# Seven-product weight sums in a one-core decoder layer: from VectorE subtractions to transfers that add in SBUF

## The chip, the cores and the metric

One NeuronCore of a Trainium2 chip runs the whole kernel. The metric is device time of one execution in microseconds (us); lower is better. The names used for the engines are those of the profile: PE (TensorE), PEld (TensorE's weight loads), DVE (VectorE), ACT (ScalarE), POOL (GpSimd), SP (SyncE), the last of which only issues transfers here.

## What is computed

One decoder layer on 256 tokens of width 2048, in float32. What matters here is the start and the end of it:

```
proj = x @ w_in                      # queries, gates, RG-LRU input, merge gates g_a, g_b, ...
attn = sparse_attention(...)         # 16 heads
branch_a = (attn * silu(attn_gate)) @ w_branch_a
branch_b = (rglru(...) * silu(rnn_gate)) @ w_branch_b
merged = sigmoid(g_a) * branch_a + sigmoid(g_b) * branch_b
x = layernorm(alpha * x + merged @ w_out)
```

The change concerns two column blocks of 512 of the merge gates: block 2 of g_a and block 3 of g_b, both products of x with 2048 x 512 pieces of w_in.

## The kernel before

Float32 products are made from three matmuls of float32r halves: `hi_of` (L115, on ACT) rounds a tile, `lo_of` (L119, on DVE) subtracts the rounded part. So every weight tile is loaded by SP into a buffer `raw` (four of them, 128 x 1024), rounded by ACT into `hi`, subtracted by DVE into `lo` (five of each), and only then used by PE. A buffer `raw` comes free when DVE has made the `lo`; SP waits for that before it issues the next load into it, and issues in program order. The list `halves` holds all weight tiles in the order of use. `load_to(n)` (L203) issues loads up to tile n, `split_to(n)` (L253) makes hi and lo; callers keep the splits about five tiles ahead of PE and the loads about nine.

The query projection runs over 32 column tiles, `single(i)`, i from 0 to 31, each with two weight tiles of kind `wt`. Attention of a head (`head(h)`) is laid between them in small steps, each in its place on the engines' queues. For each head SP loads a bias tile, POOL adds the causal mask to it (L563, two instructions), and DVE uses it (L623 and L625). DVE, ACT and POOL take their instructions strictly in program order, so an instruction that waits holds up everything behind it.

Behind most of the query tiles a step of the second seven-product group is inserted (a Strassen-like scheme: the two gate blocks are four 128-token by 1024-row by 512-column quarter products each way, computed with seven products instead of eight). The steps are j1 (k = 0 to 7), j2 (0 to 7), j3 (0 to 3), j4 (0 to 7), one for each query tile, each with one more entry in `halves`. Its weights are sums of quarters of the weight matrix, made on DVE by `sums` (L231) from what lies in `raw` and in eight lasting tiles `form[k]`, 128 x 512:

- j1: form = raw's second half - raw's first half (L240); the matrix `wj` holds both halves side by side
- j2: form = half of raw - form (L242)
- j3: raw = form - raw, in two halves (L246)
- j4: form = form - half of raw (L249)

`quarter_step` (L954) multiplies them with sums of x: SJ[1], SJ[2], SJ[4] are made before (`early_sums`), SJ[3] by four calls of `late_sum(j)` during the steps j2 and j3, as three additions on POOL each (L935 to L937) into a tile `s3d`, which ACT and DVE split. `after_j1` to `after_j4` combine the products in PSUM to the gate blocks.

Of the kernel before, what the change touches and what calls it, by code (L numbers as in the profile page):

```python
# [14 lines left out]
OP = mybir.AluOpType  # L15
# [76 lines left out]
def layer(ctx, tc, ar, out):  # L92
    nc = tc.nc
# [41 lines left out]
    def slot(name, dt=F32R, late=False):  # L135
        tag, bufs = ("late", 2) if late else ("slot", 14)
        return big.tile([P, 2 * T], dt, name=name, tag=tag, bufs=bufs)
# [44 lines left out]
    halves, where = [], {}  # L182
# [15 lines left out]
    NO = len(halves)  # L198
    halves += [("wo", ec, pc) for ec in range(4) for pc in range(8)]
    raws, parts = {}, {}  # L200
    st = {"load": 0, "split": 0}

    def load_to(n):  # L203
        while st["load"] < min(n, len(halves)):
            i = st["load"]
            kind, a, s = halves[i]
            st["load"] += 1
            if kind in ("s1b", "s2b") or kind in ("j2", "j4") and a % 2:
                continue
            if kind == "s1a":  # L210
                nc.sync.dma_start(form[a], ar["wgb"][0, 4 + a // 2, :, a % 2, :])
            raw = wpool.tile([P, 1024], F32, name=f"raw{i}", tag="raw", bufs=4)
            raws[i] = raw
            if kind == "wt":
                src = ar["wt"][a, :, s * 8:(s + 1) * 8, :].rearrange("p k c -> p (k c)")
            elif kind == "j1":
                src = ar["wj"][a].rearrange("p k c -> p (k c)")
            elif kind in ("j2", "j3", "j4"):
                src = {"j2": ar["wgb"][3, 4 + a // 2], "j3": ar["wga"][2, a], "j4": ar["wga"][2, 4 + a // 2]}[kind]
                src = src.rearrange("p k c -> p (k c)")  # L220
            elif kind in ("s1a", "s2a"):
                src = ar["ws"][a + (8 if kind == "s2a" else 0)].rearrange("p k c -> p (k c)")
            else:
                src = ar[kind][a, s].rearrange("p k c -> p (k c)")
            nc.sync.dma_start(raw, src)

    form = {}

    def sums(i):  # L231


        kind, k, _ = halves[i]
        if kind in ("j2", "j4") and k % 2:
            i = next(n for n in reversed(range(i)) if halves[n][:2] == (kind, k - 1))
        raw = raws[i]
        half = raw[:, k % 2 * 512:(k % 2 + 1) * 512]
        if kind == "j1":
            return nc.vector.tensor_sub(form[k], raw[:, 512:], raw[:, :512])  # L240
        if kind == "j2":
            return nc.vector.tensor_sub(form[k], half, form[k])  # L242
        if kind == "j3":
            for e in range(2):
                c = slice(e * 512, (e + 1) * 512)
                nc.vector.tensor_sub(raw[:, c], form[2 * k + e], raw[:, c])  # L246
            return
        if kind == "j4":
            return nc.vector.tensor_sub(form[k], form[k], half)  # L249
        nc.vector.tensor_sub(raw[:, 512:], raw[:, 512:], raw[:, :512])  # L250
        nc.vector.tensor_sub(form[k], form[k], raw[:, 512:])

    def split_to(n):  # L253
        while st["split"] < min(n, len(halves)):
            i = st["split"]
            kind, k, _ = halves[i]
            follower = halves[i + 1][0] if i + 1 < len(halves) else None
            if follower == "s1a":
                load_to(i + 2)
                sums(i + 1)  # L260
            load_to(i + 1)
            if NO + 24 <= i < NO + 28:
                raw = raws.pop(i)
                pieces = []
                for e in range(2):
                    late = i == NO + 27 and e == 1
                    hi, lo = slot(f"wh{i}_{e}", late=late), slot(f"wl{i}_{e}", late=late)
                    c = raw[:, e * 512:(e + 1) * 512]
                    hi_of(hi, c)
                    lo_of(lo, c, hi)  # L270
                    pieces.append((hi, lo))
                parts[i] = pieces
            else:
                if kind == "s1b":
                    raw = raws.pop(i - 1)
                    nc.vector.tensor_sub(raw[:, 512:], form[k], raw[:, :512])
                    src = [(slice(0, 512), form[k]), (slice(512, 1024), raw[:, 512:])]
                elif kind == "j1":
                    src = [(slice(0, 512), raws.pop(i)[:, :512]), (slice(512, 1024), form[k])]
                elif kind in ("j2", "j4"):  # L280
                    n = i if k % 2 == 0 else next(n for n in reversed(range(i)) if halves[n][:2] == (kind, k - 1))
                    raw = raws.pop(n) if k % 2 else raws[n]
                    src = [(slice(0, 512), raw[:, k % 2 * 512:(k % 2 + 1) * 512]), (slice(512, 1024), form[k])]
                elif kind == "s2b":
                    src = [(slice(0, 512), form[k])]
                else:
                    raw = raws[i] if kind == "s1a" else raws.pop(i)
                    src = [(slice(0, 1024), raw)]
                if kind == "s2a":
                    nc.vector.tensor_sub(form[k], form[k], raw[:, :512])  # L290
                hi = wpool.tile([P, 1024], F32R, name=f"hi{i}", tag="hi", bufs=5)
                lo = wpool.tile([P, 1024], F32R, name=f"lo{i}", tag="lo", bufs=5)
                for c, v in src:
                    hi_of(hi[:, c], v)
                for c, v in src:
                    lo_of(lo[:, c], v, hi[:, c])
                parts[i] = (hi, lo)
            if follower in ("j1", "j2", "j3", "j4"):
                load_to(i + 2)
                sums(i + 1)  # L300
            st["split"] += 1

    def mm(ps, w, rhs, high, start, stop):
# [369 lines left out]
    gates = {}  # L673
# [230 lines left out]
                    S[i + 1, 2 * j + e] = (dst[i][:, e, 0, :], dst[i][:, e, 1, :])  # L904


    SJ = {}

    def early_sums():

        x = yield from load_quarters(0)
        yield 8
        homes = {(s, j): slot(f"sj{s}_{j}").rearrange("p (k e t) -> p k e t", k=2, e=2)
                 for s, j in [(1, j) for j in range(4)] + [(s, j) for j in range(4) for s in (2, 4)]}
        for j in range(4):
            yield 2
            a11, a21, a12, a22 = four(x, j)
            v = {s: rows2(tmp_tile(f"sumj{j}_{s}", tag, 2)) for s, tag in ((1, "g"), (2, "g"), (4, "u"))}
            nc.vector.tensor_add(v[1], a21, a22)
            nc.vector.tensor_sub(v[2], v[1], a11)  # L920
            nc.vector.tensor_sub(v[4], a12, v[2])
            yield
            for s in v:
                hi_of(homes[s, j][:, :, 0, :], v[s])
            yield 2
            for s in v:
                lo_of(homes[s, j][:, :, 1, :], v[s], homes[s, j][:, :, 0, :])
                for e in range(2):
                    SJ[s, 2 * j + e] = (homes[s, j][:, e, 0, :], homes[s, j][:, e, 1, :])

    def late_sum(j):
# [16 lines left out]
        for i in range(2):  # L948
            SJ[3, 2 * j + i] = (hi[:, i, :], lo[:, i, :])

    psj = {}
    cq = {}

    def quarter_step(job, k):  # L954
# [4 lines left out]
        def a(row, t):  # L959
            return xs[:, row, t * P:(t + 1) * P], xs[:, row, T + t * P:T + (t + 1) * P]  # L960

        todo = {"j1": lambda: ((1, a(k, 0)), (5, SJ[1, k])),
                "j2": lambda: ((3, SJ[4, k]), (6, SJ[2, k])),
                "j3": lambda: ((7, SJ[3, 2 * k]), (7, SJ[3, 2 * k + 1])),
                "j4": lambda: ((2, a(8 + k, 0)), (4, a(8 + k, 1)))}[job]()
# [19 lines left out]
    def after_j2():  # L985

        cq["b"] = gates["ga", 2, 1] = gate_tile("ga2_1")
        nc.vector.tensor_add(cq["b"], psj[6], cq["a"])
        yield
        nc.gpsimd.tensor_add(cq["c"], cq["c"], cq["b"])  # L990
        yield 2
        gates["gb", 3, 0] = gate_tile("gb3_0")
        nc.vector.tensor_add(gates["gb", 3, 0], psj[3], cq["c"])

    def after_j3():

        nc.vector.tensor_add(cq["b"], psj[7], cq["b"])
        yield
        gates["gb", 3, 1] = gate_tile("gb3_1")
        nc.vector.tensor_add(gates["gb", 3, 1], psj[7], cq["c"])  # L1000

    def after_j4():

        c11 = gates["ga", 2, 0] = gate_tile("ga2_0")
        nc.vector.tensor_add(c11, psj[2], cq["a"])
        nc.vector.tensor_sub(cq["b"], cq["b"], psj[4])
        accs.insert(0, 3)
        auxs.append(7)
        yield 20
        for g in (c11, cq["b"]):  # L1010
            nc.scalar.activation(g, g, AF.Sigmoid)
            yield
# [338 lines left out]
    for ec in range(3):  # L1351
        pss = [acc_tile(f"pso{ec}_0"), aux_tile(f"pso{ec}_1")]
        for pc in range(8):
            n = NO + ec * 8 + pc
# [84 lines left out]
```

## Time and profile before

| | |
|---|---|
| median of 3 runs | 1013.32 us (1013.16 to 1013.74) |
| the profiled execution: its own time | 1013.73 us |
| its span in the profile | 1012.0 us |
| granted TensorE clock, mean | 0.998 of full speed |
| PE busy | 1004.2 us, 99% |
| DVE busy | 783.9 us, 77% |
| ACT busy | 597.6 us, 59% |
| POOL busy | 149.7 us, 15% |
| moved by transfers | 210.08 MB, mean 208 GB/s |

The profile is of one execution. The span runs from the first to the last instruction; the time measured from outside is 1.7 us longer. An engine's busy time leaves out waits and the issue of transfers. "lo<-raw" means an instruction that reads the tile raw and writes lo. The time from a transfer's issue to its landing holds its wait for the transfers ahead of it.

### The profile page before, as it was taken

What the parts mean: (1) busy time and instruction counts of PE and PEld (TensorE: products, weight loads), DVE (VectorE), ACT (ScalarE), POOL (GpSimd) and SP (SyncE); (2) the same over time, 40 slices, a digit from 0 to 9 for tenths busy, and PEclk for the clock granted to TensorE, in tenths of its full rate; (3) what the DMA queues carried; (4) which work ended last, traced back from release to release, by engine and by line L of the source; (5) the groups of instructions that cost most, each with busy time, mean ns of one, the idle gap of its engine ahead of it and who ended that gap; (6) DMA issues with size and microseconds to landing.
All of it is one profiled execution on the core that took longest, in us unless ns stands there. A gap on an engine that the chain in (4) does not pass through costs nothing.

```text
span 1012.0 us, 15050 instructions
## 1 busy us (share of the span) xinstructions
PE 1004.2 (99%) x5320; PEld 865.9 (86%) x5320; DVE 783.9 (77%) x1298; ACT 597.6 (59%) x1022; POOL 149.7 (15%) x182
## 2 busy tenths in 40 slices
PE   9999999999999999999999999999999999999997
PEld 8888888888888888888888888888888888888885
DVE  5578889778789988768888878888678876655685
ACT  5566656666666667566555555555985555444452
POOL 0015621110124210300000000000343320000002
PEclk9999999999999999999999999999999999999999
DMA  9745886776646565766666676555556668656652
GB/s 307 260 151 195 282 319 209 229 220 198 187 155 214 183 213 171 238 201 209 218 219 193 221 233 191 195 187 190 174 166 206 193 211 327 219 182 188 199 167 84
DMA packets 63915, 210.08 MB, mean 208 GB/s; under 512 B 6992, under 2 KB 14032, under 8 KB 62816
## 3 DMA queue, kind: packets, MB, share of 16 engines
q1 hardware_dynamic: 60512, 195.32, 60.2%
q0 software_dynamic: 2608, 12.88, 3.4%
q8 instruction: 42, 0.69, 0.3%
q10 hardware_dynamic: 720, 0.92, 0.3%
q14 instruction: 33, 0.27, 0.1%
HBM read 206.96 MB, written 6.32 MB: 211 GB/s over the span
## 4 chain that ended last, share of the span: by engine, by line
PE 97%; DVE 2%; issue 0%; ACT 0%; DVEq 0%; ACTq 0%
PE ps_q L306 16%; PE ps_ag L306 9%; PE ps_xr L306 9%; PE ps_rg L306 9%; PE ps_bb L1107 3%; PE ps_bb L1106 3%; PE ps_ba L1106 3%; PE ps_bb L1105 3%; PE ps_ba L1105 3%; PE ps_ba L1107 3%; PE psq L306 2%; PE ps_qi L306 2%; PE pso L1107 2%; PE pso L1106 2%; PE pso L1105 2%; PE ps_gb L1106 1%
## 5 line engine op out<-in xcount | busy, mean ns | idle before, releaser
L119 DVE TENSOR_TENSOR lo<-raw,hi 128x1024 fp32r<-128x1024 f32 (+1 forms) x348 | 416.2, 1202 | 179.2 <-ACT hi L115 175.3
L115 ACT ACTIVATE hi<-raw 128x1024 fp32r<-128x1024 f32 (+1 forms) x348 | 348.3, 1017 | 156.4 <-PE pso L1107 25.3
L306 PE MATMUL ps_q<-xs,hi 128*128 128x512 f32 x512 | 126.7, 391 | 0.0
L306 PEld LDWEIGHTS ps_q<-xs,hi 128*128 128x128 f32 x512 | 94.0, 188 | 18.2
L306 PEld LDWEIGHTS ps_q<-xs,lo 128*128 128x128 f32 x512 | 65.6, 191 | 2.5
L306 PE MATMUL ps_q<-xs,lo 128*128 128x256 f32 x512 | 66.4, 283 | 0.0
L563 POOL TENSOR_TENSOR bias<-bias,mask 128x256 f32<-128x256 f32 (+1 forms) x32 | 32.2, 1026 | 195.7 <-DMA bias<-dz 184.5
L306 PE MATMUL ps_ag<-xs,hi 128*128 128x512 f32 x256 | 60.0, 390 | 0.0
L306 PE MATMUL ps_xr<-xs,hi 128*128 128x512 f32 x256 | 59.6, 390 | 0.0
L306 PE MATMUL ps_rg<-xs,hi 128*128 128x512 f32 x256 | 59.5, 390 | 0.0
L306 PEld LDWEIGHTS ps_xr<-xs,hi 128*128 128x128 f32 x256 | 47.6, 188 | 9.6
L306 PEld LDWEIGHTS ps_rg<-xs,hi 128*128 128x128 f32 x256 | 47.6, 188 | 9.6
L306 PEld LDWEIGHTS ps_ag<-xs,hi 128*128 128x128 f32 x256 | 47.5, 188 | 9.5
L1105 PE MATMUL ps_bb<-hi,ub 128*128 128x512 f32 x128 | 50.4, 393 | 0.0
L1107 PE MATMUL ps_bb<-hi,ub 128*128 128x512 f32 x128 | 49.9, 390 | 0.0
L1106 PE MATMUL ps_bb<-lo,ub 128*128 128x512 f32 x128 | 49.8, 389 | 0.0
L1106 PE MATMUL ps_ba<-lo,ua 128*128 128x512 f32 x128 | 49.8, 389 | 0.0
L1107 PE MATMUL ps_ba<-hi,ua 128*128 128x512 f32 x128 | 49.8, 389 | 0.0
L1105 PE MATMUL ps_ba<-hi,ua 128*128 128x512 f32 x128 | 49.8, 389 | 0.0
L115 ACT ACTIVATE hi<-form 128x512 fp32r<-128x512 f32 x40 | 25.4, 634 | 28.0 <-PE ps_ba L1107 8.8
L778 POOL MEMSET xp<- 128x3 f32 x16 | 1.6, 101 | 254.0 <-ACT ga L1068 164.9
L1105 PE MATMUL pso<-hi,xs 128*128 128x512 f32 x96 | 37.5, 391 | 0.0
(409 smaller groups left out, 2135.2 us busy)
## 6 DMA issues: line engine op xcount, KB each, us to landing
raw<-in_wt SPq DMA_DIRECT2D x168, 512.0 KB, 4.7
raw<-in_wba SPq DMA_DIRECT2D x32, 512.0 KB, 3.8
raw<-in_wbb SPq DMA_DIRECT2D x32, 512.0 KB, 4.2
raw<-in_wo SPq DMA_DIRECT2D x32, 512.0 KB, 3.8
raw<-in_wga SPq DMA_DIRECT2D x24, 512.0 KB, 4.6
raw<-in_wgb SPq DMA_DIRECT2D x20, 512.0 KB, 4.7
raw<-in_ws SPq DMA_DIRECT2D x16, 512.0 KB, 4.3
wr<-in_wA SPq DMA_DIRECT2D x14, 424.0 KB, 4.9
```

The lines of the kernel that those rows point to most:

```text
L115: nc.scalar.activation(hi, src, AF.Copy)
L119: nc.vector.tensor_sub(lo, src, f(hi))
L306: nc.tensor.matmul(ps[:, :n], w, rhs[:, :n], start=start, stop=stop)
L563: nc.gpsimd.tensor_add(b[:, r, :W[r]], b[:, r, :W[r]], mask[:, r, :W[r]])
L778: nc.gpsimd.memset(xp[:, 0:3], 0.0)
L1105: nc.tensor.matmul(o, mh, hi, start=first and d == 0, stop=False)
L1106: nc.tensor.matmul(o, mh, lo, start=False, stop=False)
L1107: nc.tensor.matmul(o, ml, hi, start=False, stop=d == KT - 1)
```

## The change

The sums are made by transfers that POOL issues and that add what they bring to what is in SBUF (`accum_op=OP.add`). For j1 SP loads the second half of `wj` into form, and the first half into half of a raw buffer; then a transfer adds the first half onto form. For j2 and j4 a transfer adds a 128 x 512 piece of `wgb` or `wga` onto form. For j3 SP loads a tile of `wgb` (instead of `wga`) into raw and a transfer adds another tile of `wgb`, 128 x 1024, onto it. The signs in `early_sums` and in the combination are turned so that only additions are needed. A new function `sum_to` issues these transfers; `split_to(i)` calls it for three tiles beyond the one it splits.

```
+            if kind == "j1":
+                nc.sync.dma_start(form[a], flat(ar["wj"][a])[:, 512:])
...
             elif kind == "j1":
-                src = ar["wj"][a].rearrange("p k c -> p (k c)")
+                nc.sync.dma_start(raw[:, :512], flat(ar["wj"][a])[:, :512])
+                continue
             elif kind in ("j2", "j3", "j4"):
-                src = {"j2": ar["wgb"][3, 4 + a // 2], "j3": ar["wga"][2, a], "j4": ar["wga"][2, 4 + a // 2]}[kind]
-                src = src.rearrange("p k c -> p (k c)")
+                src = flat({"j2": ar["wgb"][3, 4 + a // 2], "j3": ar["wgb"][3, a], "j4": ar["wga"][2, 4 + a // 2]}[kind])
...
+    def sum_to(n):
+
+        while st["sum"] < min(n, len(halves)):
+            i = st["sum"]
+            kind, k, _ = halves[i]
+            st["sum"] += 1
+            if kind not in ("j1", "j2", "j3", "j4"):
+                continue
+            load_to(i + 1)
+            two = slice(k % 2 * 512, (k % 2 + 1) * 512)
+            to, what = {"j1": lambda: (form[k], flat(ar["wj"][k])[:, :512]),
+                        "j2": lambda: (form[k], flat(ar["wgb"][3, 4 + k // 2])[:, two]),
+                        "j3": lambda: (raws[i], flat(ar["wgb"][3, 4 + k])),
+                        "j4": lambda: (form[k], flat(ar["wga"][2, 4 + k // 2])[:, two])}[kind]()
+            nc.gpsimd.dma_start(to, what, accum_op=OP.add)
+
     def sums(i):
...
-        if kind == "j1":
-            return nc.vector.tensor_sub(form[k], raw[:, 512:], raw[:, :512])
-        if kind == "j2":
-            return nc.vector.tensor_sub(form[k], half, form[k])
-        if kind == "j3":
-            for e in range(2):
-                c = slice(e * 512, (e + 1) * 512)
-                nc.vector.tensor_sub(raw[:, c], form[2 * k + e], raw[:, c])
-            return
-        if kind == "j4":
-            return nc.vector.tensor_sub(form[k], form[k], half)
...
+            sum_to(i + 4)
             if follower == "s1a":
                 load_to(i + 2)
                 sums(i + 1)
...
-            if follower in ("j1", "j2", "j3", "j4"):
-                load_to(i + 2)
-                sums(i + 1)
```

Two lines in `early_sums` and one each in `after_j2`, `after_j3` and `after_j4` turn an addition into a subtraction or the other way round; the number of instructions stays. The order of PE and of ACT is the same before and after; DVE loses 32 instructions, SP gains 8 transfers, POOL gains 28.

POOL's queue where the steps j3 come, before (the names with bias_ are the mask additions of successive heads, s3d_ the three additions of a late_sum):

```order
L935 TENSOR_TENSOR s3d_3607<-xs 128x256
L936 TENSOR_TENSOR s3d_3607<-s3d_3607,xs 128x256
L937 TENSOR_TENSOR s3d_3607<-s3d_3607,xs 128x256
L563 TENSOR_TENSOR bias_3525<-bias_3525,mask 128x256
L563 TENSOR_TENSOR bias_3525<-bias_3525,mask 128x128
L935 TENSOR_TENSOR s3d_3672<-xs 128x256
L936 TENSOR_TENSOR s3d_3672<-s3d_3672,xs 128x256
L937 TENSOR_TENSOR s3d_3672<-s3d_3672,xs 128x256
L990 TENSOR_TENSOR cq_c<-cq_c,ga_1_3733 128x512
```

and now (line numbers are those of the changed kernel, some five higher; the numbers in the names differ by some eight):

```order
L251 DMA form_7_1481<-in_wgb 128x512
L251 DMA raw_3543<-in_wgb 128x1024
L941 TENSOR_TENSOR s3d_3616<-xs 128x256
L942 TENSOR_TENSOR s3d_3616<-s3d_3616,xs 128x256
L943 TENSOR_TENSOR s3d_3616<-s3d_3616,xs 128x256
L568 TENSOR_TENSOR bias_3533<-bias_3533,mask 128x256
L568 TENSOR_TENSOR bias_3533<-bias_3533,mask 128x128
L941 TENSOR_TENSOR s3d_3679<-xs 128x256
L942 TENSOR_TENSOR s3d_3679<-s3d_3679,xs 128x256
L943 TENSOR_TENSOR s3d_3679<-s3d_3679,xs 128x256
L251 DMA raw_3652<-in_wgb 128x1024
L996 TENSOR_TENSOR cq_c<-cq_c,ga_1_3739 128x512
```

Two adding transfers now stand ahead of the late sum and of the head's mask addition: that of the last j2 step, and that of the first j3 step (raw_3543), which has to wait until SP's load of raw_3543 has landed. The transfers of the other three j3 steps stand ahead of cq_c, of a late sum, or of both in the same way.

SP's queue at the first step j1, before:

```order
L225 DMA raw_1949<-in_wt 128x1024
L225 DMA raw_1974<-in_wj 128x1024
L225 DMA raw_1991<-in_wuv 128x1024
L225 DMA raw_2024<-in_wt 128x1024
L225 DMA raw_2055<-in_wt 128x1024
```

and now:

```order
L230 DMA raw_1949<-in_wt 128x1024
L214 DMA form_0_1474<-in_wj 128x512
L222 DMA raw_1975<-in_wj 128x512
L230 DMA raw_1993<-in_wuv 128x1024
L230 DMA raw_2026<-in_wt 128x1024
L230 DMA raw_2056<-in_wt 128x1024
```

One load of 128 x 1024 has become two of 128 x 512; the one into form goes first and needs no free raw buffer.

## Rows read from the trace of the kernel before

**Rows 1.** The page, busy time of each engine (us, share of the span, instructions).

```profile
PE 1004.2 (99%) x5320; PEld 865.9 (86%) x5320; DVE 783.9 (77%) x1298; ACT 597.6 (59%) x1022; POOL 149.7 (15%) x182
```

**Rows 2.** The chain that ended last; below, PE's longest wait beside the one at start.

```profile
PE 97%; DVE 2%; issue 0%; ACT 0%; DVEq 0%; ACTq 0%
...
PE pspT L640 <- DVE vl L119: 0.4, 1, 0.4
```

**Rows 3.** Busy times in two stretches: us; PE, PEld, DVE, ACT, POOL; clock, DMA share, GB/s.

```profile
317.00:348.00 31.00, 30.65 (x181) 26.82 (x180) 29.96 (x47) 20.74 (x43) 10.62 (x10) 1.00 0.60 188
165.00:420.00 255.00, 254.65 (x1458) 223.40 (x1457) 213.34 (x417) 169.20 (x353) 46.42 (x46) 1.00 0.64 200
```

**Rows 4.** The four lines with sums: durations ns min/median/max, first and last start.

```profile
L240 DVE TENSOR_TENSOR form<-raw x8: 684/690/1232, 173.6 to 234.6; 128x512 f32<-128x512 f32 x8
...
L242 DVE TENSOR_TENSOR form<-raw,form x8: 676/684/954, 246.8 to 302.7; 128x512 f32<-128x512 f32 x8
...
L246 DVE TENSOR_TENSOR raw<-form,raw x8: 679/683/1218, 314.2 to 341.3; 128x512 f32<-128x512 f32 x8
...
L249 DVE TENSOR_TENSOR form<-form,raw x8: 676/683/684, 347.3 to 403.1; 128x512 f32<-128x512 f32 x8
```

**Rows 5.** POOL's transfers: one line's issue durations (ns); then KB, median us to landing.

```profile
L867 POOL DMA_DIRECT2D form<-in_xT x16: 711/724/797, 118.6 to 430.6; - x16
...
DMA to landing us min/median/max: 4.6/6.7/11.9
...
form<-in_xT POOLq DMA_DIRECT2D x8, 256.0 KB, 5.4
...
y<-in_xres POOLq DMA_DIRECT2D x2, 1024.0 KB, 9.9
gb<-in_lnb POOLq DMA_DIRECT2D x1, 1024.0 KB, 18.0
```

**Rows 6.** Timeline of the step j1, k = 4: SP, ACT, DVE, PE (start, us).

```profile
198.80 3.92 SPq L225 DMA_DIRECT2D raw<-in_wt  x2
...
212.38 0.63 ACT L115 ACTIVATE hi<-form 128x512 fp32r<-128x512 f32 x1 [1.00 <-DVE form L240]
...
214.82 0.68 DVE L119 TENSOR_TENSOR lo<-form,hi 128x512 fp32r<-128x512 f32 x1
...
223.49 0.39 PE L973 MATMUL psj<-lo,xs 128*128 128x512 f32 x1
```

**Rows 7.** SP from 300 to 350 us: the j3 loads; their median landing from 296 to 350.

```profile
304.30 0.33 SPq L225 DMA_DIRECT2D raw<-in_wga  x1
...
314.32 0.33 SPq L225 DMA_DIRECT2D raw<-in_wga  x1
...
331.27 0.33 SPq L225 DMA_DIRECT2D raw<-in_wga  x1
...
raw<-in_wga SPq DMA_DIRECT2D x5, 512.0 KB, 5.4
```

**Rows 8.** Timeline of POOL ahead of j3.

```profile
296.81 0.74 POOL L935 TENSOR_TENSOR s3d<-xs 128x256 f32<-128x256 f32 x1 [2.71 <-DVE ua L665]
...
298.78 1.07 POOL L937 TENSOR_TENSOR s3d<-s3d,xs 128x256 f32<-128x256 f32 x1
309.26 1.55 POOL L563 TENSOR_TENSOR bias<-bias,mask 128x256 f32<-128x256 f32 x2 [9.41 <-DMA bias<-dz]
```

**Rows 9.** Timeline of DVE, and of ACT (last line), around j3.

```profile
309.67 0.83 DVE L623 TENSOR_TENSOR bias<-bias,lg 128x128 f32<-128x128 f32 x1
...
312.58 1.71 DVE L119 TENSOR_TENSOR lo<-raw,hi 128x1024 fp32r<-128x1024 f32 x1
...
317.83 3.50 DVE L119 TENSOR_TENSOR lo<-raw,hi 128x1024 fp32r<-128x1024 f32 x3 [0.20 <-ACT hi L115]
...
322.62 1.06 ACT L115 ACTIVATE hi<-raw 128x1024 fp32r<-128x1024 f32 x1 [0.69 <-PE pspv L660]
```

**Rows 10.** Timeline of PE: where the second and fourth j3 step need their lo.

```profile
332.30 0.39 PE L973 MATMUL psj<-lo,spare 128*128 128x512 f32 x1
...
348.31 0.39 PE L973 MATMUL psj<-lo,spare 128*128 128x512 f32 x1
```

More of the change, by code (lines that the diff above doesn't have):

```diff
@@ L200, in layer, with flat @@
     raws, parts = {}, {}
-    st = {"load": 0, "split": 0}
+    st = {"load": 0, "split": 0, "sum": 0}
+    def flat(ap):
+        return ap.rearrange("p k c -> p (k c)")
     def load_to(n):
@@ L229, in layer @@
     form = {}
+    def sum_to(n):
[12 more added lines that the diff above has]
+            nc.gpsimd.dma_start(to, what, accum_op=OP.add)
     def sums(i):
-        kind, k, _ = halves[i]
-        if kind in ("j2", "j4") and k % 2:
-            i = next(n for n in reversed(range(i)) if halves[n][:2] == (kind, k - 1))
+        _, k, _ = halves[i]
         raw = raws[i]
-        half = raw[:, k % 2 * 512:(k % 2 + 1) * 512]
-        if kind == "j1":
-            return nc.vector.tensor_sub(form[k], raw[:, 512:], raw[:, :512])
-        if kind == "j2":
-            return nc.vector.tensor_sub(form[k], half, form[k])
-        if kind == "j3":
-            for e in range(2):
-                c = slice(e * 512, (e + 1) * 512)
-                nc.vector.tensor_sub(raw[:, c], form[2 * k + e], raw[:, c])
-            return
-        if kind == "j4":
-            return nc.vector.tensor_sub(form[k], form[k], half)
         nc.vector.tensor_sub(raw[:, 512:], raw[:, 512:], raw[:, :512])
@@ L918, in early_sums @@
             v = {s: rows2(tmp_tile(f"sumj{j}_{s}", tag, 2)) for s, tag in ((1, "g"), (2, "g"), (4, "u"))}
-            nc.vector.tensor_add(v[1], a21, a22)
+            nc.vector.tensor_sub(v[1], a21, a22)
             nc.vector.tensor_sub(v[2], v[1], a11)
-            nc.vector.tensor_sub(v[4], a12, v[2])
+            nc.vector.tensor_add(v[4], a12, v[2])
             yield
@@ L989, in after_j2 @@
         yield
-        nc.gpsimd.tensor_add(cq["c"], cq["c"], cq["b"])
+        nc.gpsimd.tensor_sub(cq["c"], cq["c"], cq["b"])
         yield 2
@@ L999, in after_j3 @@
         gates["gb", 3, 1] = gate_tile("gb3_1")
-        nc.vector.tensor_add(gates["gb", 3, 1], psj[7], cq["c"])
+        nc.vector.tensor_sub(gates["gb", 3, 1], cq["c"], psj[7])
     def after_j4():
@@ L1005, in after_j4 @@
         nc.vector.tensor_add(c11, psj[2], cq["a"])
-        nc.vector.tensor_sub(cq["b"], cq["b"], psj[4])
+        nc.vector.tensor_add(cq["b"], psj[4], cq["b"])
         accs.insert(0, 3)
```

## The prediction

> **What bounds the kernel now.** I read the page first, then the chain, then who PE waits for, then the stretch in which the change acts. PE is busy 1004.2 of 1012.0 us [rows 1]; the chain that ended last is 97% PE, and the only wait of PE between its start and its last few microseconds is one of 0.35 us (0.4 in the row), for a vl that DVE makes [rows 2]. In the stretch of the seven-product steps, 165 to 420 us, PE is busy 254.65 of 255.00 us [rows 3]. Behind it DVE is busy 213 us, ACT 169, POOL 46 [rows 3]; they work ahead of PE. So work taken off DVE there can give back 0.35 us at most, and the question is whether the new transfers come late enough to use up the lead and stop PE.
>
> A measurement of this kernel can tell about 0.2% from no change, that is 2.0 us.
>
> **Part by part.**
>
> DVE loses 32 subtractions of about 0.69 us (8 each in L240, L242, L246, L249) [rows 4], 22 us of its 213. On PE's path that is worth 0 to 0.35 us; I take 0, for the wait that holds the 0.35 us is met by the j3 delay below. Turned signs: same instructions, 0.
>
> SP issues 8 transfers more at 0.33 us each, as the loads in its timeline take [rows 7]. They lie in SP's waits for free buffers: 0.
>
> All transfers together move 8 MB more (24 adding transfers of 256 KB and 4 of 512 KB). Over 255 us that is 33 GB/s on top of 200, at a DMA share of 0.64 [rows 3], so the share goes to about 0.75: no bound by itself.
>
> POOL issues 28 transfers. One issue takes 0.72 us [rows 5], together 20 us, on an engine that is busy 46 of 255: hidden, except where something waits behind them. No row shows a transfer that adds, so its time from issue to landing must be bounded. Plain transfers of POOL land 256 KB in 5.4 us late in this stretch (6.7 over the kernel), 1 MB in 9.9, at worst 18.0 [rows 5]. Between the first and the third, 512 KB would take 5.4 + (9.9 - 5.4)/3 = 6.9 us. A transfer that adds 512 KB also handles the old content, 1 MB in all: 9.9 us. I take the middle, **8.4 us for 512 KB**, and likewise 6.2 us for 256 KB (between 5.4 and 6.9); ends 5.4 and 18.0.
>
> *j1.* Take k = 4. SP can load form right behind the second weight tile of the pair that starts at 198.80, so at 202.7 [rows 6]; at 5.4 us, as for 256 KB above, it lands at 208.1. POOL then issues the adding transfer, which lands at 208.1 + 6.2 = 214.3. ACT wants this form at 212.38 [rows 6]: 1.9 us late. The lo is done at 214.82 + 0.68 = 215.5 and PE uses it at 223.49 [rows 6], so the lead is 8.0 us and covers it: 0. Without the cover (18.0 us) the lo would be 13.7 late and PE would lose 5.7.
>
> *j2 and j4.* Here form has lain in SBUF since the step before, the transfer waits for no load and stands one mask addition ahead of its use, about 8 us and more: 0. Only the first j4 step stands behind the last j3 transfer, and shifts with it.
>
> *j3* is the costly place. There raw is a ring buffer: first a load into a free buffer, then the adding transfer, then hi and lo, and each is also a stop in POOL's queue.
>
> First step. SP issues the load at 304.30 and it lands 5.4 us later [rows 7], at 309.7. POOL's queue stands until then. After the issue (0.7, to 310.4) come the three additions of s3d, which took 3.0 us from 296.81 to 299.85 while POOL was free [rows 8], so the mask addition starts at 313.4 instead of 309.26 [rows 8]: 4.1 us late. DVE's L623 waits for it, and behind it on DVE the lo that began at 312.58 and took 1.71 [rows 9], now done at 318.4. The last j2 subtraction ahead of that load is gone (0.68, [rows 4]), so all of this comes 0.6 earlier: 317.8.
>
> Second step. That lo frees the buffer; the old load went out at 314.32 [rows 7], the new at 317.8. Landing at 323.2, the addition at 331.6, hi 1.06 later [rows 9] at 332.7, lo another 1.2 (one of the three in 3.50 us [rows 9]) at 333.9. PE wants that lo at 332.30 [rows 10]: **1.6 us late**.
>
> Fourth step. Its buffer is freed by the second lo behind the second step's: 333.9 + 2.4 = 336.3 (the old load went out at 331.27 [rows 7]). Then 5.4, 8.4, 1.06 and 1.2 us: 352.4, against 348.31 [rows 10]: 4.1 us late, the 1.6 included. The third step's load follows a lo that is not held up this way and lands earlier than PE's delayed need: nothing added.
>
> The sum is +4.1 us. PE never waits later in the kernel, so nothing gives it back. Each microsecond of the 512 KB transfer counts twice, in the second and in the fourth step: nothing lost at 6.3 us, 2.0 lost at 7.4, 7.1 at 9.9, 23 at 18.0. Against the profiled execution (1013.73 us, span 1012.0) that is 1017.8; the median of the runs is 0.4 lower, so **1017.4 us**.
>
> **The rivals.**
>
> *It hides (the other side: not slower).* Place: the fourth j3 step. If 512 KB land within 7.4 us, the chain above costs PE less than 2.0 us, at 6.3 nothing, and 1013.3 comes out, or 1013.0 with the 0.35 us. For it: ACT waits for DVE at such places today [rows 6], DVE becomes lighter, and 256 KB landed in 5.4 us. Against it: the late mask addition and the chain of two transfers in a row, which no lead seen here covers with room to spare.
> The Trainium skill's page "DMA: Bandwidth & Descriptors", section "Anatomy of one DMA — SWDGE (gpsimd) path", fits a transfer issued by GpSimd as 2.0 us plus its bytes at 436 GB/s; worked out from that page, an estimate, 512 KB would take 3.2 us and this rival would hold. The trace does not agree for plain ones: 256 KB took 5.4 to 6.7 us in the median here [rows 5], where that fit gives 2.6.
>
> *The additions are as slow as the slowest row.* At 18.0 us j3 loses 23 us, and j1 starts to lose too (5.7 us at its first such step): 1036 to 1042; at 13 us it is 13, 1026.
>
> *DVE holds up POOL's issue.* If each adding transfer had to wait for the DVE instruction that runs, an issue would come up to 1.2 us later (a lo [rows 9]); counted twice in j3, +2.4: 1019.8. The longest plain issue was 0.80 us against a median of 0.72 [rows 5], with DVE busy most of the time, so little speaks for it.
> The Trainium skill's page "SBUF — State Buffer", in its box on the "DVE blocks DMA" trap, says that GpSimd cannot write descriptors while DVE runs an operation in a mode that uses both ports, and that the transfer then seems blocked; by that rule this change puts loads on the path where they can be blocked. The issue durations here show no such block.
>
> *Faster.* If unseen short waits of PE vanish with DVE's 22 us, a gain over 2.0 us would be needed; PE's 0.35 us in the stretch excludes it but for missing records.
>
> **How the numbers follow.** Chances: the j3 chain late by 2 to 9 us, 0.45 (the likeliest: 1017.4); hidden within 2.0 us, 0.35; additions much slower, 0.14; DVE holding up the issue, 0.03; faster, 0.03. So faster 0.03, same 0.35, slower 0.62. Range: the low end takes in the hidden case with its 0.35 us, 1012.9; the high end reaches into the slow case to 13 us a transfer, 1026.5. Left out are the faster case and the slower half of the slow ones, and some scatter. The likeliest case's own range is 1015.4 to 1022.
>
> **What would show it.** In the changed profile: 28 transfers of POOL with a landing time, 512 KB near 8.4 us; DVE some 22 us less busy; PE no longer without waits between 306 and 350 us but about 4 us short there, behind hi or lo of raw, and unharmed before 300; the mask addition of the head at 309 starting near 313; SP's fourth j3 load some 5 us later. The prediction is wrong if PE stops already in the steps j1 or j2, if the 512 KB transfers take under 6.3 or over 11 us, or if the time is lost after 420 us.

## The result, and the profile after

The changed kernel takes 1023.41 us (median of 4 runs, 1022.31 to 1024.99); the kernel before took 1013.53 beside it (4 runs, 1013.16 to 1014.38). The ratio is 1.0097, with a 95% interval of 1.0080 to 1.0115: 9.9 us slower. The direction was forecast; the size was forecast as 4.1 us. The profiled execution below is the slowest of the four: it took 1024.99 us, its span 1023.1.

The page, busy time of each engine and the chain that ended last:

```profile
PE 1007.4 (98%) x5320; PEld 866.5 (85%) x5320; DVE 767.9 (75%) x1266; ACT 593.8 (58%) x1022; POOL 174.2 (17%) x210
...
PE 88%; DMA 5%; DVE 3%; issue 2%; ACT 1%; POOL 0%; DVEq 0%; SPq 0%; ACTq 0%; POOLq 0%
```

DVE is 16 us less busy than in [rows 1] (22 us of sums gone, its other work longer by 6), POOL 24.5 us more, and PE now has idle time. In the chain DMA holds 5%, where [rows 2] had none.

The two stretches of [rows 3]:

```profile
317.00:348.00 31.00, 28.20 (x161) 24.22 (x160) 23.80 (x36) 15.77 (x33) 15.28 (x16) 1.00 0.77 204
165.00:420.00 255.00, 248.09 (x1406) 215.62 (x1405) 187.41 (x359) 159.09 (x338) 69.62 (x70) 0.99 0.80 224
```

PE was busy 254.65 of 255 us and now is 248.09: some 7 us of standing, in this stretch of the same length. The DMA share went from 0.64 to 0.80, the rate only from 200 to 224 GB/s: the engines work more time for each byte.

Whom PE waits for (total, times, longest; the wait at the program's start and two at its end left out):

```profile
PE pspT L645 <- ACT lg L642: 1.8, 1, 1.8
PE pspT L645 <- DVE vl L119: 1.7, 2, 1.0
PE ps_q L311 <- DVE s_q L398: 1.5, 1, 1.5
...
PE psj L978 <- ACT hi L115: 1.0, 1, 1.0
PE psj L979 <- DVE lo L119: 0.8, 1, 0.8
...
PE psj L978 <- DVE gb L1006: 0.2, 1, 0.2
```

Only 1.8 us of these 7.0 are waits for a weight's own hi or lo. The rest are waits for small pieces of other work (s_q, a product copied out of PSUM; lg of the softmax; vl; gb), which stand *behind* a hi or lo in the queues of ACT and DVE. The first such place, in j1 (ACT, two DVE rows and PE):

```profile
192.92 0.63 ACT L115 ACTIVATE hi<-form 128x512 fp32r<-128x512 f32 x1 [5.64 <-DMA form<-in_wj]
...
193.59 0.69 DVE L119 TENSOR_TENSOR lo<-form,hi 128x512 fp32r<-128x512 f32 x1 [5.58 <-ACT hi L115]
194.20 0.42 DVE L398 TENSOR_TENSOR s_q<-ps_q,r_q 128x256 f32<-128x256 f32 x1
...
194.76 2.08 PE L311 MATMUL ps_q<-xs,hi 128*128 128x512 f32 x8 [1.46 <-DVE s_q L398]
```

ACT stands 5.64 us for the adding transfer, DVE 5.58 us behind ACT. The s_q that ran at 188.67 before runs at 194.20, and PE, whose bank it empties, stops for 1.46 us, though PE does not yet need the late form.

In j3, SP's four loads, ACT's four hi, the lo of the first (the first of three in one row), the two lo ahead of the fourth load, and the lo of the last:

```profile
304.58 0.33 SPq L230 DMA_DIRECT2D raw<-in_wgb  x1
...
317.47 0.33 SPq L230 DMA_DIRECT2D raw<-in_wgb  x1
...
325.83 0.33 SPq L230 DMA_DIRECT2D raw<-in_wgb  x1
...
338.02 0.33 SPq L230 DMA_DIRECT2D raw<-in_wgb  x1
...
321.22 2.96 ACT L115 ACTIVATE hi<-raw 128x1024 fp32r<-128x1024 f32 x3 [3.87 <-DMA raw<-in_wgb]
...
330.33 1.06 ACT L115 ACTIVATE hi<-raw 128x1024 fp32r<-128x1024 f32 x1 [3.92 <-DMA raw<-in_wgb]
...
340.84 1.06 ACT L115 ACTIVATE hi<-raw 128x1024 fp32r<-128x1024 f32 x1 [1.80 <-DMA raw<-in_wgb]
...
353.40 1.06 ACT L115 ACTIVATE hi<-raw 128x1024 fp32r<-128x1024 f32 x1 [3.98 <-DMA raw<-in_wgb]
...
322.31 3.50 DVE L119 TENSOR_TENSOR lo<-raw,hi 128x1024 fp32r<-128x1024 f32 x3 [2.51 <-ACT hi L115]
...
333.83 4.16 DVE L119 TENSOR_TENSOR lo<-raw,hi 128x1024 fp32r<-128x1024 f32 x2
...
354.49 1.22 DVE L119 TENSOR_TENSOR lo<-raw,hi 128x1024 fp32r<-128x1024 f32 x1 [5.78 <-ACT hi L115]
```

Read it as a loop. The first hi waits for its transfer until 321.22; the three lo end at 325.8; at 325.83 SP gets a free buffer for the third load, 4.5 us later than the 321.36 of before. The second hi waits until 330.33 and holds up the lo that free the buffer for the fourth load: 338.02, where [rows 7] had 331.27. The fourth lo ends at 355.7.

The head's mask addition on POOL and L628, which is L623 of the kernel before, on DVE:

```profile
315.37 2.39 POOL L568 TENSOR_TENSOR bias<-bias,mask 128x256 f32<-128x256 f32 x2
...
312.31 1.62 DVE L628 TENSOR_TENSOR bias<-bias,lg 128x128 f32<-128x128 f32 x1
```

L628 starts 3 us before this mask addition, so it does not wait for it: it uses the bias of the head before, and POOL adds the mask one head ahead.

Three stretches around the fourth lo; the granted clock is the third figure from the right:

```profile
345.00:350.00 5.00, 3.96 (x21) 3.37 (x21) 3.71 (x3) 1.67 (x5) 4.63 (x4) 1.00 0.92 230
350.00:355.00 5.00, 4.05 (x24) 3.07 (x22) 0.51 (x1) 1.60 (x4) 0.00 (x0) 1.00 0.95 263
355.00:360.00 5.00, 4.24 (x12) 3.27 (x12) 5.00 (x11) 3.84 (x8) 2.33 (x3) 0.66 0.62 167
```

After PE stood for 1.8 us at 346, 0.95 at 354.5 and 0.76 at 355.8, the clock over 355 to 360 was 0.66, so part of it at 1.2 instead of 2.4 GHz: 5 x 0.34 = 1.7 us more. PE was 7.5 us behind the kernel before at the fourth j3 lo (355.77 for the 348.31 of [rows 10]), 9.3 us behind at the first j4 step and 9.7 us behind at its last matmuls (1015.00 for 1005.26).

The span grew by 11.1 us, and the last 1.4 of them lie behind PE's last matmul, at the end of the program. There POOL runs an instruction called DRAIN (its longest is the third of the three numbers, in ns; before, then now):

```profile
L1435 POOLq DRAIN  x3: 46/102/3518, 1006.5 to 1011.7; - x3
...
L1441 POOLq DRAIN  x3: 46/102/5803, 1016.3 to 1022.6; - x3
```

It is 2.3 us longer, and now it ends (1022.1) after SP is done with the output (1020.9); before, it ended first (1010.0 and 1011.2). Over all the traces of this layer its length follows the number of transfers that POOL issued, adding or not: 3.52 us with 26, 3.84 with 30, 4.17 with 34, 4.82 with 42, 5.48 with 50, 5.80 with 54, 6.13 with 58, that is 0.08 us for each. From PE's last matmul to the end of the span it took 5.5 to 5.7 us with up to 34 transfers, 5.9 with 42, 6.6 with 50, 7.2 with 54 and 58.

The transfers themselves: their issue on POOL (ns, min/median/max), and from the list of issues KB and median us to landing:

```profile
L251 POOL DMA_DIRECT2D form<-in_wj x8: 858/872/942, 169.8 to 236.9; - x8
...
L251 POOL DMA_DIRECT2D raw<-in_wgb x4: 867/876/883, 312.1 to 344.0; - x4
```

```profile
form<-in_wj POOLq DMA_DIRECT2D x8, 256.0 KB, 5.7
...
raw<-in_wgb POOLq DMA_DIRECT2D x4, 512.0 KB, 8.2
```

### The profile page after: what moved, and what is told of

It reads as the page before. It is cut to its first block, busy times and chain, and to the rows that moved or that the text cites. A ratio compares the mean times of both kernels' runs of the same rounds, so it can differ in the third digit from the quotient of the medians.

```text
span 1023.1 us, 15101 instructions
## 1 busy us (share of the span) xinstructions
PE 1007.4 (98%) x5320; PEld 866.5 (85%) x5320; DVE 767.9 (75%) x1266; ACT 593.8 (58%) x1022; POOL 174.2 (17%) x210
## 4 chain that ended last, share of the span: by engine, by line
PE 88%; DMA 5%; DVE 3%; issue 2%; ACT 1%; POOL 0%; DVEq 0%; SPq 0%; ACTq 0%; POOLq 0%
PE ps_q L311 11%; PE ps_xr L311 9%; PE ps_rg L311 9%; PE ps_ag L311 7%; PE ps_bb L1113 3%; PE ps_bb L1112 3%; PE ps_ba L1112 3%; PE ps_ba L1111 3%; PE ps_bb L1111 3%; PE ps_ba L1113 3%; DMA raw<-in_wgb 2%; DMA form<-in_wj 2%; PE psq L311 2%; PE ps_qi L311 2%; PE pso L1113 2%
## 5 line engine op out<-in xcount | busy, mean ns | idle before, releaser
L568 POOL TENSOR_TENSOR bias<-bias,mask 128x256 f32<-128x256 f32 (+1 forms) x32 | 34.4, 1092 | 123.0 <-DMA bias<-dz 122.9
L119 DVE TENSOR_TENSOR lo<-form,hi 128x512 fp32r<-128x512 f32 x40 | 27.7, 691 | 20.6 <-ACT hi L115 20.4
```

Of the source, the lines that this page charges most:

```text
L119: nc.vector.tensor_sub(lo, src, f(hi))
L568: nc.gpsimd.tensor_add(b[:, r, :W[r]], b[:, r, :W[r]], mask[:, r, :W[r]])
```

## The experiments

All times are medians beside runs of the kernel before of the same call (1013.4 to 1013.8 us).

**Which stage costs.** Three kernels put some stages' sums back on DVE, with the change's signs, and leave the others as transfers:

```
-            if kind not in ("j1", "j2", "j3", "j4"):
+            if kind not in ('j1', 'j2', 'j4'):
...
+            if follower in ('j3',):
+                load_to(i + 2)
+                sums(i + 1)
```

(this one for j3 on DVE; the others have `('j3',)` or `('j2', 'j4')` in the first line, and the rest after it.)

> The steps j3 have their sums on DVE again (two subtractions each, as before the change); j1, j2 and j4 keep their adding transfers. Theory 'two transfers in a row': in j3 and in j1 a tile needs a load, then an adding transfer, then hi and lo, and ACT and DVE stand still behind it; in the changed profile PE is 2.6 us late at the end of j1 and the rest of the 9.9 us comes from j3 on. So about +2.6 us here, 1016.1. Rival 'traffic': the 8 MB more slow all loads, and the loss goes with the bytes; 6 of 8 MB are left, so +7.4 us, 1020.9. Rival 'slow adding' (a transfer that adds takes much longer than a plain one): as the first theory, 1016.

Measured: 1016.31 us, ratio 1.0029 (1.0017 to 1.0040), +2.5.

> Only the steps j3 use adding transfers; j1, j2 and j4 have their sums on DVE. Two transfers in a row: the part of the loss that arose from j3 on, about +7 us, 1020.5. Traffic: 2 of 8 MB, +2.5 us, 1016.0. Slow adding: +7 us, as the first.

Measured: 1021.20 us, ratio 1.0077 (1.0062 to 1.0092), +7.4.

> Only the steps j2 and j4 use adding transfers, onto form tiles that have lain in SBUF for a step; j1 and j3 have their sums on DVE. Two transfers in a row: no load is waited for here, so nothing is lost, 1013.5 within 0.7. Traffic: 4 of 8 MB, +5 us, 1018.5. Slow adding: nothing, unless a transfer takes over 10 us.

Measured: 1014.01 us, ratio 1.0003 (0.9993 to 1.0012), no change.

So the loss comes with j1's transfers (2.5) and j3's (7.4), together 9.9, the whole of it; the 16 of j2 and j4 alone cost nothing. The theory that the added traffic as such slows every load is out: j2 and j4 carry half of the added bytes. Without j3's sums PE ends 1.4 us later in the profile, from a wait of 1.2 for an s_q, and 0.8 us come behind it, with 50 transfers of POOL. With j3's alone the end takes no longer; PE waits 5.6 us, for lg (3.4), gb (1.6) and a vl (0.6), and never for a hi or lo of j3 itself.

**Is it the adding?**

```
-            nc.gpsimd.dma_start(to, what, accum_op=OP.add)
+            nc.gpsimd.dma_start(to, what)
```

> The changed kernel with its 28 transfers of POOL as plain copies: the same bytes, the same places and waits, but nothing is added (the second operand of each weight sum is left as if it were the whole sum). Two transfers in a row: the chain stays; at most 1.5 us less for each of the 512 KB transfers, so 1020 to 1023.4. Slow adding: most of the loss goes, 1014 to 1016. Traffic: the same bytes from HBM, 1023.

Measured: 1015.41 us, ratio 1.0023 (1.0013 to 1.0032), +1.6. This refutes my theory that two transfers in a row are enough: with the same places, bytes read and issues, most of the loss goes when the transfers do not add. What is left is the end of the program: PE ends 0.2 us later than before in this profile, and the end behind it takes 7.2 us instead of 5.7, as in the change. In this run 512 KB landed in 5.2 us instead of 8.2, 256 KB of j1 in 3.8 instead of 5.7, and an issue took 0.55 us instead of 0.87.

**What adding costs by itself.** A kernel with transfers only. Its first part runs one transfer at a time, each behind the last:

```
        for i in range(6):
            nc.gpsimd.dma_start(t, src(i, n))
        for i in range(6):
            nc.gpsimd.dma_start(t, src(i, n), accum_op=OP.add)
```

> No part of the layer is computed: this kernel only moves 512 KB and 256 KB blocks, alone and eight at once, loaded by SP, loaded by POOL, and added by POOL, so its time is not compared. If adding is slow in itself, a 512 KB adding transfer alone lands 2 us or more behind a plain one of POOL (in the kernel the medians were 8.2 and 5.2 us), a 256 KB one 1 us or more, and eight adding transfers at once move fewer GB/s than eight plain ones. If adding is only slow in the traffic of the kernel, the two land within 0.5 us of each other when alone.

One line's instructions in a window: issue (ns), then issue to landing (us); 512 KB plain and adding, 256 KB plain and adding. The plain windows leave out each size's first transfer, which landed after 5.1 and 5.3 us:

```profile
L107 POOL DMA_DIRECT2D big<-in_wgb x5: 527/527/543, 26.3 to 42.4; - x5
...
DMA to landing us min/median/max: 3.5/3.6/4.1
...
L109 POOL DMA_DIRECT2D big<-in_wgb x6: 848/858/887, 46.2 to 73.0; - x6
...
DMA to landing us min/median/max: 5.0/5.1/5.2
...
L107 POOL DMA_DIRECT2D small<-in_wgb x5: 536/536/562, 79.1 to 92.4; - x5
...
DMA to landing us min/median/max: 2.9/3.0/3.1
...
L109 POOL DMA_DIRECT2D small<-in_wgb x6: 857/866/895, 95.7 to 116.7; - x6
...
DMA to landing us min/median/max: 3.6/3.9/4.0
```

From 256 to 512 KB a plain transfer grows by 0.6 us (437 GB/s), an adding one by 1.2 (218 GB/s): half the rate, over a start of 2.4 and 2.7 us. The plain figure is rough, since single transfers of 512 KB scatter by 0.6 us. The expectation of 2 us or more between them, alone, missed (1.5 and 0.9). The half rate shows again with eight transfers of 512 KB issued at once, in the DVE operations that each wait for one landing (plain, then adding):

```profile
143.50 0.16 DVE L120 TENSOR_TENSOR zero<-manyd,zero 128x1 f32<-128x1 f32 x1 [1.12 <-DMA manyd<-in_wgb]
144.78 0.16 DVE L120 TENSOR_TENSOR zero<-manye,zero 128x1 f32<-128x1 f32 x1 [1.13 <-DMA manye<-in_wgb]
...
163.04 0.16 DVE L120 TENSOR_TENSOR zero<-manyd,zero 128x1 f32<-128x1 f32 x1 [2.40 <-DMA manyd<-in_wgb]
165.52 0.16 DVE L120 TENSOR_TENSOR zero<-manye,zero 128x1 f32<-128x1 f32 x1 [2.32 <-DMA manye<-in_wgb]
```

One landed every 1.28 us plain (410 GB/s), every 2.5 us adding (210). The Trainium skill's page "DMA: Bandwidth & Descriptors", section "Anatomy of one DMA — SWDGE (gpsimd) path", gives 2.0 us plus the bytes at 436 GB/s: its slope is near that of the plain transfers here, which have 0.4 us more of start; adding ones have half of it.

**j1: more lead.** j3 on DVE as above, and each j1 step's form loaded and added to one step ahead:

```
             if kind == "j1":
-                nc.sync.dma_start(form[a], flat(ar["wj"][a])[:, 512:])
+                for b in ((0, 1) if a == 0 else (a + 1,) if a < 7 else ()):
+                    nc.sync.dma_start(form[b], flat(ar["wj"][b])[:, 512:])
...
+            if kind == "j1":
+                for b in ((0, 1) if k == 0 else (k + 1,) if k < 7 else ()):
+                    nc.gpsimd.dma_start(form[b], flat(ar["wj"][b])[:, :512], accum_op=OP.add)
+                continue
```

> The run without transfers in j3 (1016.3 us, 2.5 over the kernel before), with the load and the adding transfer of each j1 step issued one step (about 8 us) earlier. Theory lead: j1 loses because load, adding transfer and hi follow each other inside one step, so with a step more the loss goes: 1013.5 to 1014.5 us. Rival traffic or issue cost of j1's adding: the same bytes and issues are still there, so 1016 to 1016.5 us.

Measured: 1014.51 us, ratio 1.0011 (1.0002 to 1.0021). Of the 2.5 us 1.4 are back, just past the upper bound that I had set. All waits of ACT for a j1 form but one of 0.2 us are gone from its profile, and PE has no wait that the kernel before has not. The hi that waited 5.64 us in the change:

```profile
187.03 0.62 ACT L115 ACTIVATE hi<-form 128x512 fp32r<-128x512 f32 x1
```

Of the last 1.1 us 0.8 lie at the program's end, which takes 6.6 us behind PE's last matmul instead of 5.7, with 50 transfers of POOL; PE itself ends no later than before. So j1's wait costs some 1.5 us, and most of the rest goes with the number of transfers.

**j3: POOL's order.** j3 alone, with each adding transfer issued one tile later:

```
-            sum_to(i + 4)
+            sum_to(i + 3)
```

> Only j3's sums are transfers (1021.2 us, 7.4 over the kernel before), with the adding transfer put behind POOL's late sum and mask addition instead of ahead of them. Theory POOL order (the prediction's term for j3): ScalarE's waits for s3d of 2.4 to 4.3 us and the late mask addition go, so 1016.5 to 1018 us. Theory landing: the step is late because load and adding transfer together take 12 to 15 us before hi can start, so 1020 to 1022 us.

Measured: 1021.82 us, ratio 1.0072 (1.0056 to 1.0089). No gain, but the edit did less than the expectation says. The third and the fourth transfer moved behind a late sum; the first still goes out (310.63) ahead of the first late sum (311.29) and of the mask addition (314.95, where the run with j3 alone has 314.30). So this run does not test the first step's order on POOL. The run with own tiles, below, does: there too the first transfers go out at 310.21 ahead of the late sum, the mask addition starts at 315.40, ACT waits 5.6 us for s3d, and the loss is gone.

**j3: the order on ACT and DVE.** j3 alone, hi and lo of its block behind those of the next block:

```
+                todo = [(hi, lo, src)]
+                if kind == "j3":
+                    held.append(todo.pop())
+                else:
+                    todo += [held.pop()] if held else []
...
```

> Only j3's sums are transfers (1021.2 us), and ScalarE and VectorE make hi and lo of the j3 block after those of the block that follows it, instead of before. Theory queues in order: what costs is the work that stands behind the waiting hi on ScalarE and VectorE, so with 3 us of other work ahead of it the loss falls to 1 to 4 us: 1015 to 1018 us. Theory ring: the j3 block holds one of the four raw buffers through load and adding transfer whoever waits, so the loads behind it come late all the same: 1020 to 1022 us.

Measured: 1018.45 us, ratio 1.0045 (1.0030 to 1.0060): +5.1 instead of +7.4. It fell between the two expectations. How much of the loss is work behind the waiting hi is not shown by it: putting hi and lo back made PE wait 1.5 us for j3's own hi and lo, which it never did with j3 alone.

**j3: who owns the buffer.** j3 alone. Four tiles that j2 has done with take its blocks, in place of the ring, at the old places in the order:

```
+            if kind == "j3":
+                for b in (a,):
+                    sides[b] = [big.tile([P, 512], F32, name=f"side{b}_{e}", tag="side", bufs=4) for e in range(2)]
+                    for e, to in enumerate(sides[b]):
+                        nc.sync.dma_start(to, flat(ar["wgb"][3, b])[:, e * 512:(e + 1) * 512])
+                continue
             raw = wpool.tile([P, 1024], F32, name=f"raw{i}", tag="raw", bufs=4)
...
```

> Only j3's sums are transfers (1021.2 us, 7.4 over the kernel before), and the j3 blocks lie in two pairs of tiles of their own (four tiles that j2 has done with, so loads and adding transfers of 256 KB instead of 512 KB) in place of the ring of four raw buffers; loads and adding transfers stand where they stood in the order. Theory ring (a j3 block holds one of four buffers through load and adding transfer, and the loads behind it come late): at most 3.5 us over the kernel before, 1017 us or less. Theory lead (the adding transfer starts too late for the hi that waits for it, whoever owns the buffer): 1018.5 to 1021.5 us.

Measured: 1014.33 us, ratio 1.0005 (0.9996 to 1.0014). The loss is gone, though ACT still waits up to 2.6 us for each half of a block.

That run also halved the transfers. The same halves, back in the ring:

```
+            elif kind == "j3":
+                for e in range(2):
+                    c = slice(e * 512, (e + 1) * 512)
+                    nc.sync.dma_start(raw[:, c], flat(ar["wgb"][3, a])[:, c])
+                continue
...
```

> As the run with tiles of their own (1014.3 us, 0.6 over the kernel before), with the same loads and adding transfers of 256 KB, but the j3 blocks back in the ring of four raw buffers, as in the run with j3 alone (1021.2 us, transfers of 512 KB). Theory ring: what cost was the buffer held through load and adding transfer, so nearly all comes back: 1018.5 to 1021.5 us. Rival halves: what the tiles of their own gained came from the smaller transfers, whose first half lands early, so 1014 to 1016 us.

Measured: 1020.44 us (1016.73 to 1021.60), ratio 1.0064 (1.0039 to 1.0089). It was the ring. PE's waits with the ring (the first three lines) and with tiles of their own (the last), beside those of the kernel before:

```profile
PE pspT L669 <- ACT lg L666: 2.5, 2, 1.3
PE psj L1002 <- DVE gb L1030: 1.6, 1, 1.6
...
PE pspT L669 <- DVE vl L119: 0.8, 1, 0.8
```

```profile
PE pspT L673 <- DVE vl L119: 0.9, 1, 0.9
```

**j3: tiles of its own and a step of lead.** The same, with the load and the adding transfer of block k + 1 at the place of block k; and the whole change with this and early j1:

```
-                for b in (a,):
+                for b in ((0, 1) if a == 0 else (a + 1,) if a < 3 else ()):
```

> As the run with tiles of their own, with the load and the adding transfer of each j3 block issued one j3 step (some 10 us) earlier. Theory lead and theory ring: both causes are gone, at most 1 us over the kernel before, 1013 to 1014.5 us. Rival rate (an adding transfer keeps the DMA engines busy twice as long as a plain one, so the loads around it come late wherever it stands): 1016 us or more.

Measured: 1022.52 us, ratio 1.0090 (1.0075 to 1.0105).

> All 28 sums as transfers, as in the change, with the load and the adding transfer of j1 and j3 issued one step earlier and j3 in tiles of its own. Theory lead and ring: what is left is the 1.1 us of the run with early j1 and the remainder of j3, so 1013.5 to 1015.5 us. Rival rate: 1017 us or more.

Measured: 1023.09 us, ratio 1.0095 (1.0078 to 1.0112). Both missed by 8 us. The timeline of the first (SP, POOL, ACT), then what SP's `side` loads waited for on PE, and PE's longest wait:

```profile
302.59 12.15 SPq L222 DMA_DIRECT2D side<-in_wgb  x4
...
317.95 0.86 POOL L255 DMA_DIRECT2D side<-in_wgb  x1 [6.46 <-DMA side<-in_wgb]
...
322.35 0.42 ACT L115 ACTIVATE s3h<-s3d 128x256 fp32r<-128x256 f32 x1 [11.93 <-POOL s3d L971]
```

```profile
SPq L222 <- PE psj L1008: 10.6, 2, 10.2
...
PE pspT L673 <- DVE vl L119: 7.2, 1, 7.2
```

Loaded a step early, block 1 wants tiles that PE still reads for the last j2 step. SP stands there for 10 us with other loads behind it; POOL stands in front of the second block's transfer, with s3d behind it; ACT stands 11.93 us for s3d; DVE and then PE follow. After that wait the granted clock was 0.71 over 328 to 332 us and 0.55 over 332 to 337, which makes the other 2 us or so. A transfer issued too early into a queue that keeps its order cost as much as one issued too late. The whole change with early j1 and j3's own tiles at the *old* places was not tried; from the parts (1.1 and 0.6, and more transfers at the end) I estimate 1 to 3 us above the kernel before. None of the versions beats the kernel before, where PE has 0.35 us to give.

## Why the prediction was right and wrong

The measured 1023.41 us lies in the range as a whole, but above the likeliest case's own end of 1022, and the additions were not slower than forecast. The direction came out by the kind of delay that was forecast, hi and lo in j3's ring waiting for an adding transfer; much of the path to the number did not.

- *PE is the bound, DVE's 22 us are worth nothing*: right. No run was faster, and DVE's lower share shows nowhere in the time.
- *j1: 0, the lead of 8.0 us covers it*: this step failed; 2.5 us, of which 0.8 lie at the program's end. I compared PE's need with the late **form** alone. ACT and DVE keep their order, and behind the waiting hi and lo stood an s_q with a lead of only 4.2 us (done at 189.1 in the kernel before; PE reached it at 193.3 in the change). A lead must be taken for every instruction queued behind the waiting one. The step k = 4 that I worked out was a mild one: ACT waited 1.1 us there (forecast: 1.9), but 4.5 to 5.9 us at every other step.
- *j2 and j4: 0*: right alone (1.0003). In the change PE stands 0.7 us at 260, for a vl.
- *512 KB adding in 8.4 us*: right, 8.2; 256 KB in 6.2: 5.7 to 7.0. The issue took 0.87 us, not 0.72.
- *j3, first step: L623 waits for the late mask addition*: this failed; that path does not exist. L628 started at 312.31, the mask addition at 315.37. The rows had shown it: in [rows 8] and [rows 9] L623 starts at 309.67, while the two mask additions run from 309.26 to 310.8. The second load still went out at 317.47 (forecast 317.8), which is luck: PE was 2.6 us late from j1 and j2 by then, and L628 ran 2.6 us after the L623 of before. With j3 alone it went out at 313.78, no later than before.
- *j3, second step: lo done at 333.9, PE 1.6 us late*: it was done at 332.7, and PE never waited for it.
- *j3: "The third step's load follows a lo that is not held up this way ... nothing added"*: this failed. I let the first step delay the mask addition only, and gave its own hi no time. That hi waited until 321.22, and the lo behind it released the third load 4.5 us late (1.1 with j3 alone). The third hi came at 340.84, and PE stood 1.8 us at 346 for an lg behind it. The sum had no term for work behind a waiting hi; with j3 alone such work is all that PE waits for.
- *j3, fourth step: 352.4*: right in kind, 355.7 in size. From the second step's lo to the fourth load I took 2.4 us; it was 5.4, with 1.2 us of other DVE work in between and 4.16 for two lo that ran beside POOL's additions for s3d. The kernel before had 4.9 us there. The last transfer also took 9.3 us, not 8.4. With j3's blocks in the ring the stage cost 7.4 us, out of it 0.6.
- *PE's clock*: the sum had no term for it. In the profiled execution the short waits of PE were followed by 1.7 us at the lower clock. With j3 alone the profiled execution, the fastest of its four (1019.64 us), had a mean granted clock of 0.998, as before; the other three had 0.996 or 0.997 and took 1021.1 to 1023.1.
- *The end of the program*: the sum took POOL's issues as hidden; the last 1.4 us are the longer DRAIN.
- *What would show it wrong*: two of the signs came, PE stopping already in j1 and j2, and time lost after 420 us.
- *Rivals*: that it hides came nowhere near; that DVE holds up the issues did not show. Issues took 0.86 to 1.20 us in the kernel and 0.85 to 0.90 one at a time with DVE idle, and the 1.2 are those of a second transfer right behind a first; eight in a row with DVE idle grew from 0.88 to 3.30.

## What to carry to other kernels

A sum moved into an adding transfer is not free of the DMA's time: price it at twice the bytes, and count the buffer that it holds through load *and* addition, since in a short ring later loads start later for it (here by 4.5 and 6.8 us). When a wait is added to an engine that keeps its order, list all that is queued behind it and take the smallest lead among them, not the lead of the data that is late. Before you write that an instruction waits for another, look whether it ever starts first. Before issuing a transfer earlier, look at what its buffer still waits for: the queue stands there with everything behind it.

## What the runs showed of the hardware

Adding into SBUF ran at half the rate of a copy (218 against 437 GB/s by the growth from 256 to 512 KB, one 512 KB transfer each 2.5 us against 1.28), and its issue on POOL took 0.87 us against 0.54. In the kernel the difference grew from the 1.5 us of a 512 KB transfer alone to 3.0 us (8.2 against 5.2), at a DMA share of 0.80. Each transfer that POOL issued, adding or plain, made its DRAIN at the end 0.08 us longer (3.52 us with 26, 5.80 with 54). Two lo took 4.16 us beside POOL's additions, 2.35 with POOL idle (338.46 in the kernel before). The granted clock over 355 to 360 us was 0.66, after PE had stood 1.8, 0.95 and 0.76 us between 344 and 356.
